# A log-sum-exp kernel on one core: a written order for the last six half-tiles, a bitwise check of the sums, and a store of its own for one column of results

## The chip, the cores and the metric

The kernel runs on one core of one Trainium2 chip. The metric is the device time of one execution in microseconds; three runs of the kernel before gave 322.96, 323.04 and 323.05. Engines are named as in the profile: PE is TensorE, DVE is VectorE, ACT is ScalarE, POOL is GpSimd, SP is SyncE, which here only issues DMAs. An engine works through its own instructions in order and waits on semaphores for the others.

## The reference

`x` has 8 x 2048 x 2048 float32, `bias` 8 x 256. Each row of 2048 is 8 heads of 256. For every row and head, the log of the sum of exponentials of `x + bias` over the 256 elements is wanted, and each result stands twice in the output of 8 x 8 x 4096 float32.

```python
x_heads = x.reshape(B, S, H, Dh).transpose(0, 2, 1, 3)
x_heads = x_heads + bias[None, :, None, :]
x_tiled = np.repeat(x_heads, 2, axis=2)
mx = x_tiled.max(axis=-1, keepdims=True)
lse = mx.squeeze(-1) + np.log(np.exp(x_tiled - mx).sum(axis=-1))
```

## The kernel before

**The work.** The 16384 rows of `x` are taken in 64 tiles of 128 partitions x 2 rows x 2048 (a row of a tile is 128 x 2048 float32, 1 MB, and one head of it 128 x 256, 128 KB). "Row 62.1" is row 1 of tile 62. A batch has eight tiles, the last batch is tiles 56 to 63. The kernel sums exponentials without subtracting a maximum, and checks at the end whether the sums stayed in a safe range; if not, `all_again` (from L674) computes everything once more in the safe way. With this input it doesn't run.

**Four ways to do a head.** The bias can be added before the exponential, by TensorE: a matmul puts the bias into a PSUM bank, a second one with the identity adds `x` ("add", L831), and ScalarE takes the exponential out of PSUM, either with the sum in the same instruction ("sum", `sum_biased`, L480) or without ("copy", L842). Or the exponential is taken first, in place ("exp", `exp_inplace`, L505), and multiplied by the exponential of the bias afterwards: VectorE multiplies and sums in one instruction per head ("weigh", L540), or GpSimd multiplies (step 0, L557) and folds the head in halves down to 32 elements (steps 1 to 3, L563) and VectorE sums the rest ("folded", L570). A head that was copied out of PSUM is folded from step 1 on, without the multiplication.

**Stages.** Tiles 0 to 53 share the heads out in one way, 54 to 56 in another, 57 and up row by row (`PROMPT_F1`: two heads by TensorE, five weighed, one folded). From `T_TAIL` (62 before) on, the order is written out by hand: `TAIL_LOADS` lists the loads as (tile, row, first head, last head + 1), and `TAIL` the operations in the order in which they are issued. A word such as `weigh a:3` is head 3 of row a, and `fold a:01.1` step 1 for heads 0 and 1; a to d are the rows of `ROWS`. Since every engine is in order, this list sets the order on each engine; between engines semaphores do. `sums`, `rest`, `bits`, `limit` and `warm` stand for work left over from tile 61, for parts of the check, and for a matmul without a use of its own.

**PSUM.** Two pairs of banks (`pairs`) serve the adds in turn. `next_bias` (L800) puts the bias of the next "add" of the list into the next bank as soon as the add before it is issued. TensorE waits there until ScalarE has read what was in the bank.

**Queues.** All loads and the stores of the results of batches 0 to 6 (`store`, L601) are issued by SyncE, in order, on one queue (q1 in the profile); at most eight transfers are outstanding, since each new one waits for the one eight before it. The bias, its three bf16 parts (L316) and the last store (L750) are issued by ScalarE on another queue (q10).

**The end.** The sums of the last batch stand in `R_last`, 128 partitions x 128 columns (head, tile of the batch, row). `finish_last` (L740) transposes them on TensorE, takes the logarithm (L749) into `res_last`, and stores 128 rows of 256 float32 from ScalarE (L750). `judge` (L657) subtracts the bits of 1.0 from the bits of the last sums (L627), takes the largest absolute value with that of the earlier ones (L645), adds it up over the partitions with a matmul (L665), and changes the type (L666); every engine loads the verdict (L667) and branches (L956). The earlier sums were treated by `off_seen` on GpSimd and `limit_seen` on VectorE. Then each engine waits at the end of the program, SyncE for all outstanding transfers too (L983).

Of the kernel before, what the change touches and what calls it, by code (L numbers as in the profile page):

```python
# [40 lines left out]
ONE_BITS = 127 << 23  # L41
SPAN_BITS = 60 << 23
# [8 lines left out]
T_TAIL = 62  # L51
# [15 lines left out]

ROWS = {"a": (62, 0), "b": (62, 1), "c": (63, 0), "d": (63, 1)}


TAIL = """
add a:01  sums  add a:2  warm
exp a:3-7
rest  bits
weigh a:3  weigh a:4  weigh a:5  weigh a:6  weigh a:7
exp d:4-7
copy a:01
sum a:2
fold a:01.1  fold a:01.2  fold a:01.3
add b:2  # L80
exp b:3-7
weigh d:4  weigh d:5  weigh d:6  weigh d:7
sum b:2
add c:1
exp c:2-4
fold b:67.0  fold b:67.1  fold b:67.2  fold b:67.3
weigh b:3  weigh b:4  weigh b:5
add b:0
exp b:1
sum c:1  # L90
exp c:5-7
weigh c:2  weigh c:3  weigh c:4  weigh b:1
add c:0
sum b:0
exp d:3
folded a:01  limit
weigh c:5  weigh c:6  weigh c:7
sum c:0
exp d:1
add d:0  add d:2  # L100
weigh d:3  weigh d:1
sum d:0
sum d:2
folded b:67
# [4 lines left out]
def kernel(  # L109
# [44 lines left out]
    off = sb.tile([P, 1 + 2 + NR + H * SEEN], F32, name="off")  # L154
    off_last = sb.tile([P, H * LATE + 1], F32, name="off_last")
    far = sb.tile([P, 1], BF16, name="far")
    scale_bf = sb.tile([P, 1], BF16, name="scale_bf")
    verdict = sb.tile([1, 1], I32, name="verdict")
# [26 lines left out]
    sb.tile([P, 24], F32, name="gap")  # L185
# [19 lines left out]
    def rows_of(t, n=1):  # L205


        b, at = divmod(t, NBLK)
        if b < B - 2:
            blk, i = divmod(at, TB)  # L210
            v = x[b, blk * P * KB : (blk + 1) * P * KB, :]
            return v.rearrange("(p k) d -> p k d", k=KB)[:, i * K : (i + n) * K]
        v = x[b, at * P * K : (at + 1) * P * K, :]
# [119 lines left out]
    nc.vector.memset(Rx[0][:, 0:1], 1.0)  # L333
    nc.vector.memset(Rx[0][:, 1 + widths[0] :], 1.0)
    nc.vector.memset(off[:, 0:1], float(SPAN_BITS))
    nc.vector.memset(scale_bf, 2.0**-8)
# [32 lines left out]
    def on_bank(i, ins, banks=1):  # L369
        here = range(i, i + banks)  # L370
        for at, u in bank_users[i // 2]:
            if not set(at) & set(here) and u.ins.engine != ins.ins.engine:
                tc.declare_no_dep(ins.ins, u.ins, reason="another bank")
        bank_users[i // 2].append((here, ins))
        return ins
# [176 lines left out]
    def fold_step(t, k, h0, h1, step, after):  # L552


        v = xts[t % NBUF][:, k, h0 * Dh : h1 * Dh]
        if step == 0:
            done = nc.gpsimd.tensor_tensor(  # L557
                out=v, in0=v, in1=w_sb[:, h0 * Dh - W1 : h1 * Dh - W1], op=ALU.mult
            )
            return on_x(t, done, [after])  # L560
# [5 lines left out]
        return on_x(t, done, [after])  # L566

    def add_folded(t, k, h0, h1, sums, done):
        v = xts[t % NBUF][:, k, h0 * Dh : h1 * Dh]
        red = nc.vector.tensor_reduce(  # L570
            out=sums[:, k, h0:h1],
            in_=v.rearrange("p (h j) -> p h j", j=Dh)[:, :, 0:FOLD],
            op=ALU.add,
            axis=mybir.AxisListType.X,
        )
        on_x(t, red, [done])

    def fold(t, k, h0, h1, sums, after):
        step = 0
        while Dh >> step >= FOLD:  # L580
            after = fold_step(t, k, h0, h1, step, after)
            step += 1
        return lambda: add_folded(t, k, h0, h1, sums, after)
# [42 lines left out]
    def off_one(engine, to, bits):  # L626
        engine.tensor_scalar(  # L627
            out=to,
            in0=bits,
            scalar1=-1.0 * ONE_BITS,  # L630
            scalar2=None,
            op0=ALU.add,
        )
# [4 lines left out]
    def off_seen():  # L638
        n = 1 + 2 + NR
        off_one(nc.gpsimd, off[:, 1:n], Rx[len(groups)].bitcast(I32))  # L640
        to = off[:, n:].rearrange("p (h c) -> p h c", h=H)
        off_one(nc.gpsimd, to, last_bits(0, SEEN))

    def farthest(to, of):
        nc.vector.tensor_reduce(  # L645
            out=to,
            in_=of,
            op=ALU.max,
            axis=mybir.AxisListType.X,
            apply_absolute_value=True,  # L650
        )

    def limit_seen():
        n = H * LATE
        farthest(off_last[:, n : n + 1], off)

    def judge():  # L657


        n = H * LATE  # L660
        to = off_last[:, 0:n].rearrange("p (h c) -> p h c", h=H)
        off_one(nc.vector, to, last_bits(SEEN, NBLK * K))
        farthest(far, off_last)
        total = tp[0:1, 0, 0:1]
        nc.tensor.matmul(total, lhsT=far, rhs=scale_bf, start=True, stop=True)  # L665
        nc.vector.tensor_copy(verdict, total)  # L666
        return nc.values_load(  # L667
            verdict,
            min_val=0,
            max_val=(1 << 31) - 1,  # L670
            skip_runtime_bounds_check_because="it is only compared, and addresses nothing",
        )
# [67 lines left out]
    def finish_last():  # L740
        bank = n_ps[0] % len(ps)
        last = ps[bank][:, 0:P]
        nc.tensor.transpose(
            out=last, in_=R_last.rearrange("p h n k -> p (h n k)"), identity=ident
        )
        tv = bass.AP(
            tensor=last.tensor, offset=last.offset, ap=[last.ap[0], [1, P], [0, 2]]
        )
        nc.scalar.activation(out=res_last, in_=tv, func=ACT.Ln)  # L749
        nc.scalar.dma_start(  # L750
            out=out[B - 1].rearrange("h (n r) -> (h n) r", r=2 * P),
            in_=res_last.rearrange("q p r -> q (p r)"),
        )


    def sums_of(t):

        b, blk = divmod(t, NBLK)
        if b < B - 2:
            return R[b][:, blk % TB * K :, :, blk // TB]  # L760
        if b == B - 2:
            return R[b][:, :, :, blk]
        return R_last[:, :, blk, :].rearrange("p h k -> p k h")
# [20 lines left out]
    for word in TAIL.replace("  ", "\n").split("\n"):  # L784
# [5 lines left out]
        if "-" in heads:  # L790
            heads = [h for h in range(int(heads[0]), int(heads[-1]) + 1)]
        else:
            heads = [int(h) for h in heads]
# [5 lines left out]

    def next_bias():  # L800
        if not to_bias:
            return
        row, heads = to_bias.pop(0)

        if len(heads) > 1:
            n_ps[0] += n_ps[0] % 2
        bank = n_ps[0] % len(ps)
        n_ps[0] += 1
        n = len(heads) * Dh
# [14 lines left out]
    def tail_step(what, t, k, heads, step):  # L824
# [4 lines left out]
        if what == "add":  # L829
            bank, c = biased[(t, k), heads[0]]  # L830
# [4 lines left out]
            next_bias()  # L835
        if what == "sum":
            (h,) = heads
            bank, c = biased[(t, k), h]
            sum_biased(t, k, h, bank, in_ps(bank, c, Dh), made["add", t, k, h], sums)
        if what == "copy":  # L840
            bank, c = biased[(t, k), heads[0]]
            act = nc.scalar.activation(out=v, in_=in_ps(bank, c, n), func=ACT.Exp)  # L842
            mms = [made["add", t, k, h] for h in heads]
            on_bank(bank, on_x(t, act, mms), banks=(c + n + MM - 1) // MM)
# [6 lines left out]
        if what == "weigh":  # L851
            (h,) = heads
            weigh(t, v, h, dst, made["exp", t, k, h])
        if what == "fold":
            after = made.get(("fold", t, k, heads[0])) or made["exp", t, k, heads[0]]
            done = fold_step(t, k, heads[0], heads[-1] + 1, step, after)
            made["fold", t, k, heads[0]] = done
        if what == "folded":
            add_folded(t, k, heads[0], heads[-1] + 1, sums, made["fold", t, k, heads[0]])

    for t in range(T_TAIL):
# [4 lines left out]
        for k0, k1, c0, c1 in pieces(t):  # L866
# [6 lines left out]
            else:  # L873
                heads = add_x(m, t, k0, c0, c1, bias_here)

                def pe_part(t=t, heads=heads, sums=sums):
                    for k, h, bank, p, mm in heads:
                        sum_biased(t, k, h, bank, p, mm, sums)

            if not m["late"]:  # L880
                if next_units:
                    bias_there = put_bias(*next_units.pop(0))
                else:
                    next_bias()
# [10 lines left out]
            if h0 < h1 and not m["late"]:  # L895
# [5 lines left out]
                if hf < h1:  # L901
                    for_pool.append(fold(t, k0, hf, h1, sums, done))
# [25 lines left out]
            else:  # L928
                for_pe.append(pe_part)
# [9 lines left out]
        if t == T - 3:  # L939
            store()  # L940
    for what, row, heads, step in tail:
        if row is None:
            {
                "sums": lambda: flush(for_pe),
                "rest": lambda: flush(for_pool),
                "bits": off_seen,
                "limit": limit_seen,
                "warm": keep_warm,
            }[what]()
            continue  # L950
        tail_step(what, *row, heads, step)
    finish_last()
    again = judge() > SPAN_BITS // 2

# [33 lines left out]
```

## Time and profile before

| what | us |
|---|---|
| median of three runs | 323.04 |
| the profiled execution | 322.96 |
| its span, first to last instruction | 321.2 |
| DVE / ACT / POOL / PE busy, of the span | 286.9 / 264.2 / 287.2 / 246.3 |
| last issue of a load (SP) | 309.3 |
| last sum on ACT / on DVE ends | 317.20 / 317.57 |
| verdict written (DVE L666) | 318.50 |

The span is the time from the first to the last instruction; 1.8 us of the execution lie around it. The profile is one execution; times within it are counted from the start of the span. In a timeline the columns are: start, duration, engine, line, operation, what it writes and reads, count, and in brackets how long the engine stood idle before and who released it. An instruction's duration reaches into the next one's where the engine overlaps them, so the cost of one in a row of them is the distance from start to start. In the DMA view of a stretch, a queue's line gives its packets, MB, and the time of its packets as a share of 16 engines over the stretch. "DMA to landing" is from the issue to the last semaphore increment.

### The profile page before, as it was taken

The numbers are of one execution on the slowest core, as the hardware profiler recorded it, in microseconds if no ns is written. First come the engines' busy times: TensorE is split into PE (matmuls) and PEld (weight loads), VectorE is DVE, ScalarE is ACT, GpSimd is POOL, SyncE is SP. The second block draws the span as 40 slices with busy tenths as digits, with TensorE's granted clock in tenths as the row PEclk, the third lists the DMA queues.
The fourth block names the chain that finished last, engine by engine and source line by source line (L and its number), as shares of the span: only waits on it lengthen the run. The fifth ranks groups of instructions, "written<-read, shape, count | busy, mean of one in ns | idle before, by whom it ended". The sixth has DMA issues, their size and how long they took to land.

```text
span 321.2 us, 2277 instructions
## 1 busy us (share of the span) xinstructions
PE 246.3 (77%) x611; PEld 99.2 (31%) x612; DVE 286.9 (89%) x308; ACT 264.2 (82%) x436; POOL 287.2 (89%) x118
## 2 busy tenths in 40 slices
PE   5998787867866979866697786677877688398873
PEld 2333332323322323322233332232333233143331
DVE  1339998799999699999979999999999999999986
ACT  1169868888888697988869998889888998999995
POOL 7939997999999999999999999999999999977773
PEclk9999977999997897999869999999999999979998
DMA  7999999999999999999999999999999999999994
GB/s 297 460 420 457 400 450 443 404 457 437 412 457 417 428 451 400 453 441 413 449 434 420 449 418 433 424 426 431 433 435 432 422 435 432 417 429 427 426 411 188
DMA packets 8806, 135.44 MB, mean 422 GB/s; under 512 B 980, under 2 KB 1495, under 8 KB 2519
## 3 DMA queue, kind: packets, MB, share of 16 engines
q1 hardware_dynamic: 8640, 135.14, 98.4%
q10 hardware_dynamic: 152, 0.14, 0.1%
q8 instruction: 5, 0.08, 0.1%
q14 instruction: 9, 0.07, 0.1%
HBM read 134.23 MB, written 1.05 MB: 421 GB/s over the span
## 4 chain that ended last, share of the span: by engine, by line
DMA 48%; POOL 15%; DVE 14%; ACT 10%; PE 10%; issue 0%; SPq 0%; DVEq 0%
DMA xb<-in_x_dram 48%; POOL xb L499 15%; DVE R L524 10%; ACT xb L505 6%; PE pair L449 4%; PE one_ps L449 2%; DVE xb L540 2%; ACT xb L467 2%; DVE xb L517 2%; PE pair L391 1%; PE pair L321 1%; ACT xb L460 1%; PE one_ps L391 1%; DMA brow<-in_bias_dram 1%; ACT xb L480 0%
## 5 line engine op out<-in xcount | busy, mean ns | idle before, releaser
L499 POOL TENSOR_TENSOR xb<-xb,b_rep 128x2048 f32<-128x2048 f32 x57 | 257.6, 4547 | 19.0 <-DMA xb<-in_x_dram 18.9
L524 DVE TENSOR_REDUCE R<-xb 128x14 f32<-128x3584 f32 (+1 forms) x57 | 216.8, 3803 | 2.5 <-ACT xb L505 0.6
L505 ACT ACTIVATE xb<-xb 128x2560 f32<-128x2560 f32 (+5 forms) x78 | 156.3, 2014 | 19.1 <-POOL xb L499 19.0
L449 PE MATMUL pair<-xb,ident 128*128 128x512 f32 x216 | 109.5, 632 | 0.0
L449 PE MATMUL one_ps<-xb,ident 128*128 128x512 f32 x108 | 62.4, 662 | 16.3 <-DMA xb<-in_x_dram 16.2
L467 ACT ACTIVATE xb<-pair 128x1024 f32<-128x1024 f32 x54 | 55.5, 1028 | 17.5 <-PE pair L449 17.5
L449 PEld LDWEIGHTS pair<-xb,ident 128*128 128x128 f32 x216 | 44.3, 205 | 57.9 <-issue 57.9
L517 DVE TENSOR_TENSOR xb<-xb,w_ps 128x512 f32<-128x512 f32 x54 | 36.7, 680 | 21.2 <-ACT xb L505 21.1
L391 PE MATMUL one_ps<-b,ones_bf 128*128 128x512 bf16 x52 | 20.1, 387 | 39.8 <-ACT xb L460 39.7
L460 ACT ACTIVATE xb<-one_ps 128x256 f32<-128x256 f32 x108 | 39.9, 378 | 7.1 <-PE one_ps L449 7.1
L391 PEld LDWEIGHTS <-ones_bf 128*128 128x128 bf16 (+1 forms) x174 | 17.6, 101 | 88.4 <-issue 81.8
L391 PE MATMUL pair<-b,ones_bf 128*128 128x512 bf16 x104 | 31.2, 381 | 0.0
L449 PEld LDWEIGHTS one_ps<-xb,ident 128*128 128x128 f32 x108 | 19.6, 199 | 31.4 <-DMA xb<-in_x_dram 25.2
L426 PE MATMUL pair<-xb,ident 128*128 128x512 f32 x32 | 18.5, 679 | 8.2 <-DMA xb<-in_x_dram 8.2
L540 DVE CUSTOM_DVE_ANT_0 xb<-xb,w_ps 128x256 f32<-128x256 f32 x61 | 22.5, 417 | 0.4 <-ACT xb L505 0.4
L460 ACT ACTIVATION_READ_ACCUMULATOR xb<-one_ps 128x1 f32 x108 | 22.0, 204 | 0.0
L563 POOL TENSOR_TENSOR xb<-xb 128x128 f32<-128x128 f32 (+3 forms) x36 | 13.5, 375 | 3.9 <-ACT xb L842 1.1
L480 ACT ACTIVATE xb<-pair 128x256 f32<-128x256 f32 x39 | 15.0, 407 | 0.0
L557 POOL TENSOR_TENSOR xb<-xb,w_sb 128x256 f32<-128x256 f32 (+1 forms) x11 | 8.5, 777 | 3.7 <-ACT xb L505 3.0
L426 PEld LDWEIGHTS pair<-xb,ident 128*128 128x128 f32 x32 | 5.7, 205 | 16.8 <-DMA xb<-in_x_dram 14.8
L480 ACT ACTIVATION_READ_ACCUMULATOR xb<-pair 128x1 f32 x39 | 9.1, 233 | 0.0
L440 PE MATMUL tp<-b_rep,ident 128*128 128x384 f32 x22 | 8.9, 486 | 0.0
(64 smaller groups left out, 82.0 us busy)
## 6 DMA issues: line engine op xcount, KB each, us to landing
xb<-in_x_dram SPq DMA_DIRECT2D x20, 4096.0 KB, 22.4
xb<-in_x_dram SPq DMA_DIRECT2D x17, 2048.0 KB, 21.9
xb<-in_x_dram SPq DMA_DIRECT2D x11, 1024.0 KB, 22.1
xb<-in_x_dram SPq DMA_DIRECT2D x2, 512.0 KB, 17.5
xb<-in_x_dram SPq DMA_DIRECT2D x1, 768.0 KB
xb<-in_x_dram SPq DMA_DIRECT2D x2, 256.0 KB, 10.5
out_dram<-res SPq DMA_DIRECT2D x1, 512.0 KB
xb<-in_x_dram SPq DMA_DIRECT2D x1, 384.0 KB, 13.2
```

The lines of the kernel that those rows point to most:

```text
L391: nc.tensor.matmul(p, lhsT=lhsT, rhs=each_row(b, h * Dh, Dh, K), start=i == 0, stop=False,)
L426: mm = nc.tensor.matmul(p, lhsT=ident, rhs=xts[t % NBUF][:, ka:kb, c : c + w], start=False, stop=True,)
L449: mm = nc.tensor.matmul(p, lhsT=ident, rhs=xts[t % NBUF][:, :, h * Dh : (h + 1) * Dh], start=False, stop=True,)
L460: act = nc.scalar.activation(out=xts[t % NBUF][:, k, 0:Dh], in_=got[0][:, k * Dh : (k + 1) * Dh], func=ACT.Exp, accum_out=sums[:, k, 0:1],)
L467: act = nc.scalar.activation(out=xts[t % NBUF][:, :, Dh : m["pe"] * Dh].rearrange("p k (h j) -> p h k j", j=Dh), in_=got[-1].rearrange("p ...
L480: act = nc.scalar.activation(out=xts[t % NBUF][:, k, h * Dh : (h + 1) * Dh], in_=p, func=ACT.Exp, accum_out=sums[:, k, h : h + 1],)
L499: add = nc.gpsimd.tensor_tensor(out=v, in0=v, in1=each_row(b_rep, c - G0, D - c, k1 - k0), op=ALU.add)
L505: return on_x(t, nc.scalar.activation(out=v, in_=v, func=ACT.Exp), [after])
L517: mul = nc.vector.tensor_tensor(out=f, in0=f, in1=each_row(w_ps, m["pe"] * Dh - W0, n, k1 - k0), op=ALU.mult,)
L524: red = nc.vector.tensor_reduce(out=sums[:, k0:k1, h0:H], in_=v.rearrange("p k (h j) -> p k h j", j=Dh), op=ALU.add, axis=mybir.AxisListTy ...
L540: ttr = nc.vector.tensor_tensor_reduce(out=v, in0=v, in1=w, scale=1.0, scalar=0.0, op0=ALU.mult, op1=ALU.add, accum_out=dst,)
L563: done = nc.gpsimd.tensor_tensor(out=v[:, :, 0:n], in0=v[:, :, 0:n], in1=v[:, :, n : 2 * n], op=ALU.add)
```

## The change

- `T_TAIL` is 61 instead of 62: the written order now covers rows 61.0 to 63.1, six rows named e, f, a, b, c, d, with 14 loads where tile 61 had two and the list ten. Row c is now 63.1 and row d 63.0; the last head to arrive is head 0 of row d. Sums, copies, folds and products are shared out anew among the engines. A new word `whole` is a plain reduction on VectorE of a head that was copied out of PSUM.
- `next_bias` looks whether the bank that is next has been read by all that the list lets read it (`to_read`), and otherwise waits for a later word of the list; it is tried after every word.
- The blocks of the last batch are read in reverse order (`rows_of`, `sums_of`), so that row d's head 0 is column 0 of the sums.
- The check: a bitwise AND and a bitwise XOR in one VectorE instruction per group of sums (`odd_bits`) leave zero where a sum's top bits are the usual ones. `gather` adds the results, read as bf16, over the partitions with matmuls of at most 128 columns into one PSUM row: the earlier sums at `seen`, the last in `judge`. One reduction with absolute values gives the verdict, which is read as an integer. GpSimd's part, `limit_seen` and the change of type are gone.
- The end: `finish_last` is gone. `finish_one` takes the logarithm of column 0 as it stands, 128 partitions x 1, and stores it from ScalarE, two floats per partition. `finish_rest` transposes the other 127 columns, takes their logarithm, and stores 127 rows of 256 float32 from SyncE. In the list `final` (the first) stands ahead of `main` (the second), and both ahead of `judge`.
- `store` is called after the loop; on SyncE's queue it stands behind all loads, as before. Two memsets of the start go, two have another value; tile sizes and the unused tile `gap` change.

```diff
-T_TAIL = 62
+T_TAIL = 61
...
 TAIL_LOADS = [
-    (62, 0, 0, 8),
-    (63, 1, 4, 8),
-    (62, 1, 2, 8),
-    (63, 0, 1, 5),
-    (62, 1, 0, 2),
-    (63, 0, 5, 8),
+    (61, 0, 0, 8),
+    (61, 1, 0, 5),
+    (63, 1, 0, 8),
+    (61, 1, 5, 8),
+    (62, 0, 0, 6),
+    (62, 1, 5, 8),
+    (63, 0, 2, 7),
+    (62, 1, 0, 1),
+    (62, 0, 6, 8),
+    (62, 1, 1, 3),
+    (62, 1, 3, 5),
+    (63, 0, 1, 2),
+    (63, 0, 7, 8),
     (63, 0, 0, 1),
-    (63, 1, 0, 1),
-    (63, 1, 3, 4),
-    (63, 1, 1, 3),
 ]
...
+ROWS = {"e": (61, 0), "f": (61, 1), "a": (62, 0), "b": (62, 1), "c": (63, 1), "d": (63, 0)}
...
+add e:01  exp e:34567
+add e:2  copy e:01  weigh e:3  exp f:234  add f:01  warm
+fold e:01.1  weigh e:4  weigh e:5  copy e:2
+weigh e:6  fold e:01.2  sums  weigh e:7  copy f:01  fold e:01.3  weigh f:2
+sums  weigh f:3  fold f:01.1  exp c:34567  weigh f:4
+add c:12  whole e:2  fold f:01.2  folded e:01  rest  seen6
+fold f:01.3  exp f:567  seen7  weigh c:3  fold c:67.0  add c:0  weigh c:4
+sum c:1  weigh c:5  seen  sum c:2  weigh f:5
+copy c:0  weigh f:6  add a:12  exp a:345  fold c:67.1  weigh f:7
+whole c:0  exp b:567  folded f:01  fold c:67.2  weigh a:3  add a:0
+weigh a:4  fold c:67.3  copy a:12  weigh a:5  weigh b:5  sum a:0
+fold a:12.1  weigh b:6  add d:2  exp d:3456  weigh b:7
+fold a:12.2  add b:0  folded c:67  exp a:67  weigh d:3  fold d:6.0
+weigh d:4  sum d:2  add b:12  weigh d:5  sum b:0  fold a:12.3  weigh a:6
+exp b:34  fold d:6.1  weigh a:7  sum b:1  add d:1  folded a:12  fold d:6.2
+weigh b:3  exp d:7  weigh b:4  fold d:6.3  add d:0  sum b:2  weigh d:7
+sum d:1  folded d:6  sum d:0
+final  main
...
-    nc.vector.memset(off[:, 0:1], float(SPAN_BITS))
-    nc.vector.memset(scale_bf, 2.0**-8)
...
+    def odd_bits(to, bits):
+        nc.vector.tensor_scalar(
             out=to,
             in0=bits,
+            scalar1=TOP_BITS,
+            scalar2=USUAL_BITS,
+            op0=ALU.bitwise_and,
+            op1=ALU.bitwise_xor,
         )
...
+    odd_ps = tp[0:1, KB - 1]
+
+    def gather(bits, start, stop):
+        v = bits.bitcast(BF16)
+        n = v.shape[1]
+        for c in range(0, n, P):
+            w = min(P, n - c)
+            nc.tensor.matmul(
+                odd_ps[:, 0:w],
+                lhsT=ones_bf[:, 0:1],
+                rhs=v[:, c : c + w],
+                start=start and c == 0,
+                stop=stop,
+            )
+
+    def see_before():
+        odd_bits(odd[:, 0 : 2 + NR], Rx[len(groups)].bitcast(I32))
+
+    def see_early():
+        to = odd[:, 2 + NR :].rearrange("p (h c) -> p h c", h=H)
+        odd_bits(to, last_bits(LATE, NBLK * K))
+
+    def judge():
+        to = odd_last.rearrange("p (h c) -> p h c", h=H)
+        odd_bits(to, last_bits(0, LATE))
+        gather(odd_last, False, True)
         nc.vector.tensor_reduce(
+            out=verdict,
+            in_=odd_ps,
             op=ALU.max,
             axis=mybir.AxisListType.X,
             apply_absolute_value=True,
         )
...
-    def finish_last():
+    def finish_rest():
         bank = n_ps[0] % len(ps)
...
+        n = P - 1
+        rest = ps[bank][0:n, 0:P]
+        nc.tensor.transpose(out=rest, in_=sums_in[-1][:, 1:], identity=ident)
         tv = bass.AP(
...
+        nc.scalar.activation(out=res_last[0:n], in_=tv, func=ACT.Ln)
+        nc.sync.dma_start(
+            out=out[B - 1].rearrange("h (n r) -> (h n) r", r=2 * P)[1:],
+            in_=res_last[0:n].rearrange("q p r -> q (p r)"),
+        )
+
+    def finish_one():
+        one = sums_in[-1][:, 0:1]
+        tv = bass.AP(tensor=one.tensor, offset=one.offset, ap=[one.ap[0], [0, 2]])
+        nc.scalar.activation(out=res_one, in_=tv, func=ACT.Ln)
         nc.scalar.dma_start(
+            out=out[B - 1, 0, 0 : 2 * P].rearrange("(p r) -> p r", r=2), in_=res_one
         )
...
     def next_bias():
-        if not to_bias:
+        bank = n_ps[0] % len(ps)
+        if not to_bias or ahead or to_read[bank]:
             return
         row, heads = to_bias.pop(0)
...
+        if what == "whole":
+            red = nc.vector.tensor_reduce(
+                out=dst, in_=v, op=ALU.add, axis=mybir.AxisListType.X
+            )
+            on_x(t, red, [made["exp", t, k, heads[0]]])
...
-    finish_last()
-    again = judge() > SPAN_BITS // 2
+    again = judge() > 0
```

More of the change, by code (lines that the diff above doesn't have):

```diff
@@ L40 @@
 BIAS_MAX = 20.0
[L41 to L42 removed]
+TOP_BITS = -(1 << 28)
+USUAL_BITS = 1 << 30
 TOO_FAR = 3.0e38
@@ L153 @@
     LATE = NBLK * K - SEEN
[L154 to L158, printed above, removed]
+    odd = sb.tile([P, 2 + NR + H * SEEN], I32, name="odd")
+    odd_last = sb.tile([P, H * LATE], I32, name="odd_last")
+    verdict = sb.tile([1, 1], F32, name="verdict")
     starts = [0]
@@ L367, with on_bank @@
     bank_users = [[], []]
[L369 to L372, printed above, removed]
+    def on_bank(i, ins):
+        for j, u in bank_users[i // 2]:
+            if j != i and u.ins.engine != ins.ins.engine:
                 tc.declare_no_dep(ins.ins, u.ins, reason="another bank")
-        bank_users[i // 2].append((here, ins))
+        bank_users[i // 2].append((i, ins))
         return ins
@@ L559, in fold_step @@
             )
-            return on_x(t, done, [after])
+            return on_x(t, done, after)
         v = v.rearrange("p (h j) -> p h j", j=Dh)
@@ L565, in fold_step @@
         )
-        return on_x(t, done, [after])
+        return on_x(t, done, after)
     def add_folded(t, k, h0, h1, sums, done):
@@ L575, in add_folded @@
         )
-        on_x(t, red, [done])
+        on_x(t, red, done)
     def fold(t, k, h0, h1, sums, after):
@@ L651, in farthest @@
         )
[L653 to L666, printed above, removed]
         return nc.values_load(
-            verdict,
+            verdict.bitcast(I32),
             min_val=0,
@@ L789 @@
         heads, _, step = heads.partition(".")
[L790 to L793, printed above, removed]
+        heads = [int(h) for h in heads]
         tail.append((what, ROWS.get(row), heads, int(step or 0)))
@@ L829, in tail_step @@
         if what == "add":
+            next_bias()
+            assert ahead.pop() == ((t, k), heads)
             bank, c = biased[(t, k), heads[0]]
@@ L842, in tail_step @@
             act = nc.scalar.activation(out=v, in_=in_ps(bank, c, n), func=ACT.Exp)
-            mms = [made["add", t, k, h] for h in heads]
-            on_bank(bank, on_x(t, act, mms), banks=(c + n + MM - 1) // MM)
+            on_bank(bank, on_x(t, act, [made["add", t, k, heads[0]]]))
+            to_read[bank] -= len(heads)
             for h in heads:
@@ L853, in tail_step @@
             weigh(t, v, h, dst, made["exp", t, k, h])
+        if what == "whole":
[3 more added lines that the diff above has]
+            on_x(t, red, [made["exp", t, k, heads[0]]])
         if what == "fold":
-            after = made.get(("fold", t, k, heads[0])) or made["exp", t, k, heads[0]]
+            after = [made["exp", t, k, h] for h in heads]
+            if ("fold", t, k, heads[0]) in made:
+                after = [made["fold", t, k, heads[0]]]
             done = fold_step(t, k, heads[0], heads[-1] + 1, step, after)
@@ L858, in tail_step @@
         if what == "folded":
-            add_folded(t, k, heads[0], heads[-1] + 1, sums, made["fold", t, k, heads[0]])
+            done = made["fold", t, k, heads[0]]
+            add_folded(t, k, heads[0], heads[-1] + 1, sums, [done])
     for t in range(T_TAIL):
@@ L874, with pe_part @@
                 heads = add_x(m, t, k0, c0, c1, bias_here)
-                def pe_part(t=t, heads=heads, sums=sums):
-                    for k, h, bank, p, mm in heads:
-                        sum_biased(t, k, h, bank, p, mm, sums)
+                pe_parts = [
+                    lambda t=t, one=one, sums=sums: sum_biased(t, *one, sums)
+                    for one in heads
+                ]
+                def pe_part(pe_parts=pe_parts):
+                    flush(pe_parts)
             if not m["late"]:
@@ L901 @@
                 if hf < h1:
-                    for_pool.append(fold(t, k0, hf, h1, sums, done))
+                    for_pool.append(fold(t, k0, hf, h1, sums, [done]))
             flush(for_pe)
@@ L938, with sum_before @@
             finish_two()
-        if t == T - 3:
-            store()
+    store()
+    last_bank = heads[0][2]
+    to_read[last_bank] = len(for_pe)
+    def sum_before():
+        for_pe.pop(0)()
+        to_read[last_bank] -= 1
+    next_bias()
     for what, row, heads, step in tail:
@@ L943 @@
             {
-                "sums": lambda: flush(for_pe),
+                "sums": sum_before,
                 "rest": lambda: flush(for_pool),
-                "bits": off_seen,
-                "limit": limit_seen,
+                "seen6": see_before,
+                "seen7": see_early,
+                "seen": lambda: gather(odd, True, False),
                 "warm": keep_warm,
+                "main": finish_rest,
+                "final": finish_one,
             }[what]()
-            continue
-        tail_step(what, *row, heads, step)
-    finish_last()
-    again = judge() > SPAN_BITS // 2
+        else:
+            tail_step(what, *row, heads, step)
+        next_bias()
+    assert not for_pe and not for_pool and not to_bias
+    again = judge() > 0
     order.__exit__(None, None, None)
```

83 lines of the change are left out of this document (16 added, 67 removed).

## The prediction

> **What bounds the kernel now.** I read the page's table of DMA first, then the chain that ended last, then the timeline of ScalarE and TensorE over the last ten microseconds, then the waits of SyncE and the DMA view of the first 20 and last 5 us. The page:
>
> ```profile
> DMA  7999999999999999999999999999999999999994
> ...
> DMA packets 8806, 135.44 MB, mean 422 GB/s; under 512 B 980, under 2 KB 1495, under 8 KB 2519
> ...
> q10 hardware_dynamic: 152, 0.14, 0.1%
> ```
>
> The 16 DMA engines are full until the last slice, so the body runs at the rate of the loads, and the change touches neither their bytes nor the work up to tile 60. What it can move lies behind about 303 us. The end, from the timelines of ScalarE and TensorE:
>
> ```profile
> 316.31 0.44 ACT L480 ACTIVATE xb<-pair 128x256 f32<-128x256 f32 x1
> 316.57 0.26 ACT L480 ACTIVATION_READ_ACCUMULATOR xb<-pair 128x1 f32 x1
> 316.67 0.45 ACT L480 ACTIVATE xb<-pair 128x256 f32<-128x256 f32 x1
> 316.93 0.27 ACT L480 ACTIVATION_READ_ACCUMULATOR xb<-pair 128x1 f32 x1
> 318.06 0.38 ACT L749 ACTIVATE res_last<-pair 128x256 f32<-128x256 f32 x1 [0.85 <-PE pair L743]
> 318.47 0.39 ACTq L750 DMA_DIRECT2D out_dram<-res_last  x1
> ...
> 315.60 0.70 PE L831 MATMUL pair<-xb,ident 128*128 128x256 f32 x2
> 317.72 0.30 PE L743 MATMUL pair<-ident,R 128*128 128x128 f32 x1 [1.43 <-DVE R L570]
> ```
>
> The last load is in at 315.6 (the matmul at 315.60 starts on it). ScalarE is done at 317.20, VectorE's last sum at 317.58; transpose, logarithm and the store's issue at 318.47 follow. The store lands 1.8 us after its issue, and 0.9 us of barrier follow: 318.47 + 1.8 + 0.9 = 321.2, the span. That the store and not the verdict ends the run is in SyncE's waits, where the verdict's path (read at 318.5) is through before it:
>
> ```profile
> SPq L667 <- DVE verdict L666: 5.0, 1, 5.0
> SPq L983 <- PEq L983: 0.6, 2, 0.5
> SPq L983 <- DMA out_dram<-res_last: 0.3, 1, 0.3
> ```
>
> So whatever delays the landing of the last store delays the end one for one, and there is nothing behind which it can hide.
>
> **The new stores: how many engines they use.** The old last store has 128 rows of 1 KB. The new one leaves out row 0 (head 0 of tile 63, row half 0): 127 rows of 1 KB, on SyncE's queue. The DMA view of the last 5 us and of the first 20 us, ScalarE's queue q10 alone:
>
> ```profile
> q10 hardware_dynamic: 144, 0.13, 7.7%
> ...
> q10 hardware_dynamic: 8, 0.01, 0.3%
> ```
>
> The first is the 128-row store: 128 packets of data and 16 small ones, one for each engine that took part. The second is two transfers of one row (the bias) and three rows (its bf16 parts): 4 packets of data and 4 small ones, that is 1 and 3 engines. The page fits: SyncE issues 60 transfers of 64 or 128 rows (20+17+11+2+1+2+1+3 loads, 3 stores), 60 x 16 + 16 + 1 + 3 = 980, exactly the packets under 512 B. Every transfer whose rows I can count shares them evenly: 128 as 16 x 8, 64 as 16 x 4, 3 as 3 x 1, 1 as 1 x 1. 127 is prime: the only even share on at most 16 engines is all 127 rows on one. No row of the trace has a row count that 16 doesn't divide and that is above 16, so this cost has two ends: shared nearly as 128 rows (8 on the busiest engine), no added cost; or 127 on one. I take one engine, because even shares are the one pattern that all 63 transfers keep, and the three-row store, which left 13 engines idle rather than cut a row, is the nearest odd count.
>
> [...]
>
> Price of a 1 KB packet: 7.7% of 16 engines over 5 us is 6.16 us for 128 packets and 16 small ones, about 47 ns each. On one engine the store has 127 - 8 = 119 more of them in a line: 119 x 47 ns = 5.6 us. Bounds: at the rate of the large loads (135.14 MB in 98.4% of 16 x 321.2 us, 38 ns per KB) 4.5 us; at the rate of the small transfers at the start (0.3% of 16 x 20 us = 0.96 us for 12.5 KB, 77 ns per KB) 9.2 us.
>
> The other new store (128 rows of 8 bytes, ScalarE's queue) has 16 engines and is issued earlier; its packets are shorter than 1 KB, so I give it at most the 1.8 us of the old one. It is covered by the store that follows.
>
> **When the 127-row store is issued.** ScalarE does the exponentials of the tail without a break in both lists, so I compare lists from 303.30 on (both start with an exp of row 61.0). Start to start in the timeline, a sum costs 0.36 us, a copy of 512 columns 0.48 (310.50 to 310.98), an exp 0.10 + 0.215 per head (0.31 for one, 1.16 for five). Before: 13 sums, one copy of 512, 10 exps with 35 heads. After: 11 sums, three copies of 512, two of 256 (0.28 each, my estimate between the 0.26 that the sum's ACTIVATE takes and 0.31), 10 exps with 31 heads. Difference: -2 x 0.36 + 2 x 0.48 + 2 x 0.28 - 4 x 0.215 = -0.06 us. So ScalarE's last sum, now head 0 of the last row, is done at 317.15. Its data are in time: the list has 14 loads for 12, four of one head for three, and a 1 KB packet costs 47 ns where 1 KB of a large one costs 38, 8 per engine, so some 0.15 us later than 315.60; with the matmul's 0.70 that is 316.45, and ScalarE reaches this sum at 316.6.
>
> Then on ScalarE, one behind another: the logarithm of one column (0.25, from the 0.38 of 256 columns less most of its length), the issue of the small store (0.39, as L750), the logarithm of the 127 rows (0.38): 317.15 + 0.04 + 0.25 + 0.39 + 0.38 + 0.03 = 318.25, where SyncE issues. The transpose that the second one needs waits for the other 127 sums. VectorE ends these earlier: 28 products for 31 (0.343 each, -1.0), two reductions of one head (0.3 each), three more small folded sums (0.13), two bit operations of 130 and 80 elements (between 0.18, the old 32-wide one, and 0.55, GpSimd's 130-wide one, so 0.4 to 1.0 for both), without the reduction to a limit (0.30): about even in work, but not waiting for the final sum, it ends near 316.9. TensorE gets the added matmuls of the check: 4 of at most 128 columns, between 0.1 and 0.38 each (the 512-column bf16 row): at the upper end row 62.0's add is late by up to 1 us, which ScalarE could feel as 0.4 us; I take 0 and keep 0.4 for the range. GpSimd's folds (five chains) leave idle time.
>
> The check: one reduction and one small type change less, verdict about 0.5 us sooner. The read of the verdict was covered by the store already (the 0.3 us above), so it is worth nothing. SyncE now issues the store before it reads the verdict, 0.4 to 0.5 us later; with the store on one engine that too is covered, otherwise both ways end together. The output stores behind the loads and the two memsets less at the start cost nothing: the queue has drained by 317.8 (old landings 5 us after 311.1 to 313.0), and VectorE's first work waits for data. The rows of the last batch are read in reverse order, the same bytes.
>
> **Sum.** Issue -0.2 us (318.47 to 318.25), landing +5.6: +5.4 us. The profiled execution took 322.96 us (span 321.2 and 1.8 around it), the median is 323.04, within 0.1. 322.96 + 5.4 = **328.4 us**, span 326.6.
>
> **Rivals.**
> 1. *127 rows spread over all engines, seven or eight each.* For it: nothing in the trace forbids an uneven share. Against: none is seen. Then the landing is 1.8 us after 318.25, and the time is 322.96 - 0.2 = 322.8: not slower. What decides is one count, the small packets of that store, 16 or 1. Chance 0.10, of which 0.02 for a list that gains more than 0.65 us.
> 2. *The list itself runs dry.* ScalarE waits where a load or an add is late (six adds of the tail wait for loads in the profile before, 4.6 us in all), with the store spread. It has to lose 0.85 us to end over 0.65 slower: 323.8. Chance 0.03.
> 3. *The store isn't one transfer of 127 rows*, but cut in two (64 and 63 rows, say; 63 shares as 9 x 7). It would land under half a microsecond later than the old one: 323.3. Chance 0.02.
> 4. *One engine* (my forecast): chance 0.85.
>
> **How the numbers follow.** A difference under 0.2% (0.65 us) is about what a measurement of this kernel can't tell from no change. Slower: 0.85 + 0.03 = 0.88; within: 0.08 of rival 1 and rival 3, 0.10; faster: 0.02. The range is that of the one-engine case: the packet's bounds give 322.96 - 0.2 + 4.5 = 327.3 and 322.96 - 0.2 + 9.2 = 332.0; ScalarE's list may add 0.4 or take 0.3. 327.0 to 332.0 holds nearly all of 0.85, so about 8 in 10.
>
> **What would show it.** The DMA view of the last microseconds: SyncE's queue with 127 packets of 1 KB and one small one behind them, a share of about one sixteenth (0.06) for some 6 us, and "DMA to landing" of the new store near 7.4 us where the old had 1.8. SyncE's (or another queue's) last long wait is for res_last, 5 us or more, and all engines are idle behind 318.7. ScalarE's last sum ends within 0.4 us of 317.15, the store is issued within 0.5 of 318.25, the verdict is there before 318.2. I am wrong if that store lands within 2.5 us of its issue; then the time is near 322.8. I am wrong on the list if ScalarE shows idle gaps that sum to over 0.5 us between 303 and 317.

## The result, and the profile after

The changed kernel takes 328.82 us (median of 6 runs, 328.44 to 329.76) against 323.05 (322.93 to 323.33): a ratio of 1.0182, interval 1.0171 to 1.0193. It is 5.8 us slower; forecast was 328.4. The profiled execution is the longest of the six, 329.76 us with a span of 328.0, so its profile shows 6.8 us more than the one before, a microsecond more than the medians do.

The page after, the table of DMA and the packet counts:

```profile
DMA  7999999999999999999999999999999999999970
...
DMA packets 9222, 135.44 MB, mean 413 GB/s; under 512 B 1141, under 2 KB 1783, under 8 KB 3063
...
q10 hardware_dynamic: 152, 0.01, 0.0%
```

The loads fill the engines as before; the last slice, of 8.2 us, is nearly empty now, where before it stood at 4 tenths. The small packets can be counted again: SyncE issues 59 loads and 3 stores of results with 16 small packets each (992), ScalarE's three transfers have 16 + 1 + 3 = 20, the new store of one column brings 128 pieces of 8 bytes, and 992 + 20 + 128 = 1140. One is left for the store of 127 rows: it ran on one engine. SyncE's queue alone, from 318.5 to 327 us, says the same, 127 packets of data and one small one:

```profile
q1 hardware_dynamic: 128, 0.13, 5.1%
```

The DMA view from 318 us to the end (40 slices of a quarter of a microsecond, then packets, MB, share of 16 engines):

```profile
GB/s 25 8 0 0 4 0 0 12 8 57 20 37 12 12 25 25 25 4 0 25 25 20 25 25 25 25 25 25 25 25 25 20 25 12 0 0 0 0 0 0
...
q10 hardware_dynamic: 144, 0.00, 0.8%
...
out_dram<-res_last SPq DMA_DIRECT2D x1, 127.0 KB
out_dram<-res_one ACTq DMA_DIRECT2D x1, 1.0 KB, 4.2
```

From 319.8 to 326.4 us the core moves some 20 GB/s on average and 25 in most slices, with one engine at work on the store; the old store ran at 262 to 360 from 319.4 to 319.75. The last column is the time from issue to landing: the 8-byte store took 4.2 us, though it is 1 KB in all. The view gives none for the 127-row store, since it works from 16 increments of a transfer's semaphore and this one has fewer. The trace keeps their times, though: the 128-row store of before had 16 increments, from 320.04 to 320.23, and this one has two, one at 319.46, ahead of its first packet, and one at 326.71. SyncE's waits say the same:

```profile
SPq L1009 <- DMA out_dram<-res_last: 6.1, 1, 6.1
SPq L743 <- ACT res_last L742: 3.5, 1, 3.5
```

SyncE reached the barrier's waits at 320.5 and stood 6.1 us for the store, where the old one cost it 0.3. The store was issued at 319.02 and landed at 326.71: 7.7 us, where it was 1.8. ScalarE's end shows when it could be issued (L465 is the sum, L753 the logarithm of the column, L742 that of the 127 rows):

```profile
317.43 0.39 ACT L465 ACTIVATE xb<-pair 128x256 f32<-128x256 f32 x1
317.69 0.22 ACT L465 ACTIVATION_READ_ACCUMULATOR xb<-pair 128x1 f32 x1
317.94 0.20 ACT L753 ACTIVATE res_one<-R 128x2 f32<-128x2 f32 x1
318.17 0.39 ACTq L754 DMA_DIRECT2D out_dram<-res_one  x1
318.61 0.38 ACT L742 ACTIVATE res_last<-pair 127x256 f32<-127x256 f32 x1 [0.47 <-PE tp L633]
...
317.96 0.38 PE L738 MATMUL pair<-ident,R 128*127 128x128 f32 x1 [0.70 <-ACT xb L465]
```

The 6.8 us of the two profiles, then: the last store is issued at 319.0 instead of 318.47 (0.55), takes 7.7 us instead of 1.8 (5.9), and the end follows 1.25 us behind its landing instead of 0.95 (0.3). The waits named on the last two lines mislead a little. The second logarithm is put down to a matmul of the check, but ScalarE was issuing the small store until 318.56. The transpose does wait for ScalarE, and for the last head's sum, which it doesn't read.

### The profile page after: what moved, and what is told of

It reads as the page before. It is cut to its first block, busy times and chain, and to the rows that moved or that the text cites. A ratio compares the mean times of both kernels' runs of the same rounds, so it can differ in the third digit from the quotient of the medians.

```text
span 328.0 us, 2286 instructions
## 1 busy us (share of the span) xinstructions
PE 248.3 (76%) x618; PEld 100.1 (31%) x618; DVE 287.4 (88%) x303; ACT 264.7 (81%) x437; POOL 287.6 (88%) x118
## 4 chain that ended last, share of the span: by engine, by line
DMA 57%; POOL 22%; ACT 7%; DVE 6%; PE 3%; SPq 1%; issue 0%; ACTq 0%
DMA xb<-in_x_dram 57%; POOL xb L484 22%; ACT xb L490 5%; DVE R L509 5%; PE pair L434 2%; PE one_ps L434 1%; DVE xb L502 1%; ACT xb L465 1%; ACT xb L452 1%; SPq L234 0%; ACT xb L445 0%; DVE R L604 0%; PE one_ps L309 0%; SPq L249 0%; ACT xb L847 0%
## 5 line engine op out<-in xcount | busy, mean ns | idle before, releaser
L490 ACT ACTIVATE xb<-xb 128x2560 f32<-128x2560 f32 (+6 forms) x78 | 155.3, 2000 | 18.9 <-POOL xb L484 18.3
L548 POOL TENSOR_TENSOR xb<-xb 128x128 f32<-128x128 f32 (+3 forms) x39 | 15.5, 400 | 4.8 <-ACT xb L847 2.0
L465 ACT ACTIVATE xb<-pair 128x256 f32<-128x256 f32 x37 | 14.0, 397 | 0.0
L836 PE MATMUL pair<-xb,ident 128*128 128x256 f32 (+1 forms) x24 | 9.5, 490 | 2.3 <-DMA xb<-in_x_dram 2.3
L542 POOL TENSOR_TENSOR xb<-xb,w_sb 128x256 f32<-128x256 f32 (+1 forms) x10 | 7.8, 784 | 3.0 <-ACT xb L490 2.5
L465 ACT ACTIVATION_READ_ACCUMULATOR xb<-pair 128x1 f32 x37 | 8.3, 224 | 0.0
```

The source lines that it names most:

```text
L465: act = nc.scalar.activation(out=xts[t % NBUF][:, k, h * Dh : (h + 1) * Dh], in_=p, func=ACT.Exp, accum_out=sums[:, k, h : h + 1],)
L490: return on_x(t, nc.scalar.activation(out=v, in_=v, func=ACT.Exp), [after])
L548: done = nc.gpsimd.tensor_tensor(out=v[:, :, 0:n], in0=v[:, :, 0:n], in1=v[:, :, n : 2 * n], op=ALU.add)
```

## The experiments

The kernel before was run beside each (322.98 to 323.02 us in these sets). Ratios are to it; the two kernels with one run have none. Where a landing is given "by the increments", it is the time of the last increment in the trace.

**The 127 rows cut in two.** The changed kernel with

```diff
-            out=out[B - 1].rearrange("h (n r) -> (h n) r", r=2 * P)[1:],
-            in_=res_last[0:n].rearrange("q p r -> q (p r)"),
+        rows = out[B - 1].rearrange("h (n r) -> (h n) r", r=2 * P)[1:]
+        for q0, q1 in ((0, 112), (112, 127)):
+            nc.sync.dma_start(
+                out=rows[q0:q1],
+                in_=res_last[q0:q1].rearrange("q p r -> q (p r)"),
```

> The changed kernel, its 127-row store cut into 112 and 15 rows, two transfers on SyncE's queue. Theory (rows are shared out evenly, the engines taken are a divisor of the row count): 16 and 15 engines, the second store lands within 2.5 us of its issue, where the 127 rows took 7.7; the time falls by about 5 us to 322.8 if the 8-byte store (4.2 us from issue to landing in the changed kernel) was only held up by the 127-row one, and to 324.2 if its 4.2 us are its own, since it is then the last to land. Rival (the list, the check or the two stores as such cost the time): within 1 us of 328.8.

Measured: 325.46 us, ratio 1.0074 (1.0061 to 1.0088). 3.4 us of the 5.8 are gone, which the rival excludes; but it stops short of both values of the theory. The DMA view from 317.2 to 323 us (slices of 0.145 us; q14 fetches instructions):

```profile
GB/s 71 14 0 0 0 0 2 6 0 0 0 0 92 240 275 149 177 14 56 0 0 0 0 0 0 0 0 0 0 0 7 0 0 0 0 0 0 0 0 0
...
q14 instruction: 2, 0.02, 4.3%
...
out_dram<-res_last SPq DMA_DIRECT2D x1, 112.0 KB
out_dram<-res_one ACTq DMA_DIRECT2D x1, 1.0 KB, 4.1
out_dram<-res_last SPq DMA_DIRECT2D x1, 15.0 KB, 3.9
```

The 8-byte store's 4.1 us don't come from the 127-row store, then. And the two others, issued 0.8 and 1.3 us behind it, took 4.2 (by the increments) and 3.9 us for 7 and 1 packets on an engine, which was not expected. Nearly all their packets had started by 319.8, as the first row shows; what is late is the landing, from 321.6 to 322.5, behind the last of the 8-byte store's at 321.4.

**125 and 2 rows.** The same with the cut at 125.

```diff
-        for q0, q1 in ((0, 112), (112, 127)):
+        for q0, q1 in ((0, 125), (125, 127)):
```

> The changed kernel, its 127-row store cut into 125 and 2 rows. Theory of divisors: 125 = 5 x 25, five engines, so 25 packets of about 50 ns in a line instead of 7 in the cut at 112: the store lands about 0.9 us later than there, near 3 us after its issue, and the time is 0 to 0.9 us above that kernel's. Rival (any row count above 16 that 16 doesn't divide goes on one engine): within 0.5 us of the changed kernel, 328.8. Rival (shared unevenly over all engines): as the cut at 112.

Measured: 325.61 us, ratio 1.0079 (1.0064 to 1.0094), 0.15 above the cut at 112. SyncE's queue in the DMA view from 318 to 325.5 us, of this kernel and then of the cut at 112:

```profile
q1 hardware_dynamic: 134, 0.13, 5.8%
```

```profile
q1 hardware_dynamic: 158, 0.13, 6.0%
```

Both have 127 packets of data. The small ones left are 7 here and 31 there: 5 + 2 engines for 125 and 2 rows, 16 + 15 for 112 and 15. So the number of engines is a divisor of the rows, and not "16 or one". The 0.9 us expected for 25 packets in a line did not show at the end: the last packet started at 320.46, where with the cut at 112 all but one had started by 319.75, but the store landed 4.1 us after its issue, nearly as the 112 rows did, hidden in the same delay behind the 8-byte store.

**The old end on the new list.** The written list, the bitwise check and all else of the changed kernel, with `finish_last` of before:

```diff
-final  main
+last
...
-                "main": finish_rest,
-                "final": finish_one,
+                "last": finish_last,
```

> The changed kernel with the end of before: all 128 columns are transposed, logged and stored in one store of 128 rows from ScalarE; the written list and the bitwise check stay. Theory: no store on one engine is left, so the time is 322.3 to 323.0, and what it differs by from before (323.05) is the list and the check alone. Rival (the list costs the time): near 328.

Measured: 322.95 us, ratio 0.9999 (0.9990 to 1.0008): the two stores are the whole loss, and list and check together are worth nothing that shows. Yet in its profile, of an execution of 322.75 us, the last store was issued at 317.81, 0.66 us earlier than before. SyncE's waits at its end:

```profile
SPq L661 <- DVE verdict L654: 3.2, 1, 3.2
SPq L1023 <- DMA out_dram<-res_last: 0.9, 1, 0.9
```

The landing is at 319.56, the end at 320.88: 1.32 us behind it, where before it was 0.96. So 0.36 of the 0.66 us went behind the landing.

**The 127-row store alone, in the kernel before.**

```diff
-        nc.scalar.dma_start(
-            out=out[B - 1].rearrange("h (n r) -> (h n) r", r=2 * P),
-            in_=res_last.rearrange("q p r -> q (p r)"),
-        )
+        rows = out[B - 1].rearrange("h (n r) -> (h n) r", r=2 * P)
+        for q0, q1 in ((1, P), (0, 1)):
+            nc.scalar.dma_start(
+                out=rows[q0:q1],
+                in_=res_last[q0:q1].rearrange("q p r -> q (p r)"),
+            )
```

> The kernel before with one edit: its last store of 128 rows is cut into rows 1 to 127 and row 0, both from ScalarE. Theory: the 127 rows go on one engine, 119 packets of 52 ns more in a line, 6.2 us: 329.2, and the store lands 7.5 to 8 us after its issue where it took 1.8. Rival (the store alone is harmless, the list costs the time): 323.1 to 323.5.

Measured: 328.54 us, ratio 1.0167 (1.0153 to 1.0181). One row taken out of a store of 128, and stored by itself behind it, costs 5.5 us in a kernel that is otherwise the old one. The DMA view from 318.4 to 327 us, and SyncE's wait:

```profile
q10 hardware_dynamic: 130, 0.13, 4.7%
```

```profile
SPq L985 <- DMA out_dram<-res_last: 5.0, 1, 5.0
```

130 packets are 127 + 1 of data and two small ones: one engine each. By the increments the 127 rows landed 7.1 us after their issue and the one row 0.2 us behind them. 7.14 is 5.4 more than the 1.76 of before, at 119 packets more 45 ns each, a little under the 52 that I expected from the changed kernel.

**The column as one row.** The cut at 112, and head 0's column transposed first and stored as one row of 1 KB:

```diff
-        one = sums_in[-1][:, 0:1]
...
+        nc.tensor.transpose(out=one, in_=sums_in[-1][:, 0:1], identity=ident)
...
-            out=out[B - 1, 0, 0 : 2 * P].rearrange("(p r) -> p r", r=2), in_=res_one
+            out=out[B - 1, 0:1, 0 : 2 * P], in_=line
```

> The kernel with the store cut at 112, and the column of its own transposed first, so that it is stored as one row of 1 KB instead of 128 pieces of 8 bytes; all else as there. Theory (the 8-byte pieces are slow to land and hold up what the same engines write behind them, 2.5 us of 325.46 against 322.95 with the old end): the 112-row store lands about 2 us after its issue instead of 4.2, the one-row store within 2.5; the transpose and the longer logarithm cost up to 0.6: 323.2 to 324.0. Rival (a second small store on another queue costs it, whatever its form): 325 to 326.

Measured: 324.59 us, ratio 1.0053 (1.0037 to 1.0068). By the increments the row landed 1.1 us after its issue and the 112 rows 1.9 after theirs, where with the 8-byte pieces it was 4.1 and 4.2. So the form of the small store is what held the others up. The instruction fetches show it too: two of 8 KB took 4.0 us together with the 8-byte store (4.3% of 16 engines over 5.8 us, above) and 0.8 here (5.5 us):

```profile
q14 instruction: 2, 0.02, 0.9%
```

The time is 0.6 above the range expected: the column's logarithm now waits for a transpose and the big store is issued at 318.65 in this profile, and of the two transfers the 15-row one is the last, issued 0.4 us later still and 2.4 us on its way:

```profile
out_dram<-res_last SPq DMA_DIRECT2D x1, 15.0 KB, 2.4
```

**The big store ahead of the small one.** The cut at 112, with `main  final` for `final  main` in the list; one run.

> The kernel with the store cut at 112, and the store of the 127 columns issued ahead of the 8-byte store instead of behind it. Theory (the 8-byte writes hold up those behind them on the same engines): the 112-row store lands about 2 us after its issue instead of 4.2, the 8-byte store still some 4 us after its own, the time stays at 325.0 to 326.0. Rival (SyncE's queue is slow here by itself): 4 us for the 112 rows in either order.

Measured: 327.21 us, above the 325.0 to 326.0 expected. In this execution the transpose waited for VectorE until 318.27, and both queues issued at nearly the same time, 319.06 and 319.16, so the order asked for was hardly there. By the increments, 11 of the 112-row store's 16 came within 1.7 us, the other five after 2.3 to 4.8:

```profile
out_dram<-res_one ACTq DMA_DIRECT2D x1, 1.0 KB, 4.9
out_dram<-res_last SPq DMA_DIRECT2D x1, 15.0 KB, 4.5
```

That most of one store came early and the rest late speaks against a queue that is slow by itself. That the 8-byte writes delay what the same engines write is the author's estimate; the views don't tell the engines apart. The question of the order stays open.

**The transpose into another pair of banks.** The changed kernel; one run:

```diff
     def finish_rest():
-        bank = n_ps[0] % len(ps)
+        bank = (n_ps[0] + 1) % len(ps)
```

> The changed kernel, one edit: the transpose of the 127 columns goes to a bank of the other pair than the last head's add. Theory (in the changed kernel the transpose waited for the last head's sum, 0.70 us, although it doesn't read it, because its bank lies in the pair that this sum reads): it now starts when head 1's sum is written, about 0.35 us ahead of the end of the last head's sum, and the time stays within 0.6 us of 328.8, since ScalarE takes the small logarithm and the small store first. Rival (the sums' tile is tracked as a whole): the transpose still starts after the last head's sum.

Measured: 328.35 us, span 326.6. TensorE and ScalarE at its end:

```profile
316.75 0.35 PE L738 MATMUL pair<-ident,R 128*127 128x128 f32 x1 [0.41 <-ACT xb L465]
...
316.78 0.21 ACT L465 ACTIVATION_READ_ACCUMULATOR xb<-pair 128x1 f32 x1
```

The transpose now starts 0.24 us ahead of the end of the last sum (316.99), where it started behind it. The wait came from the shared pair. It brings nothing, since ScalarE's two earlier steps stand in front of the logarithm anyway. This execution, which doesn't have the profiled one's late loads, also shows the plain sizes: issue at 318.10, 7.2 us to the landing.

**Where the 0.66 us of the list went.** SyncE waits for the eight transfer semaphores at the end in a fixed order, 0.06 us from one to the next where all have come. Transfers take them in turn, so how many come before decides which one the last store gets: in the kernel before the seventh of the order, in the changed kernel the second, with the new list and the old end the first. Two kernels move it to the last place by leaving out one transfer; both have the new list, the new check and the old end. In the first, heads 0 and 1 to 2 of row 62.1 come in one load behind 62.0's last:

```diff
-    (62, 1, 0, 1),
     (62, 0, 6, 8),
-    (62, 1, 1, 3),
+    (62, 1, 0, 3),
```

> The list and the check of the changed kernel with the end of before, and one load less (62.1 heads 0 and 1 to 2 in one transfer behind 62.0 heads 6 to 7). Theory: that kernel's last store was issued 0.66 us earlier than before's (317.81 against 318.47) and the time stayed the same, since SyncE, which waits for the eight transfer semaphores in a fixed order of some 0.06 us each, had seven waits still to do behind the store's where before had one; one transfer less moves the store to the last semaphore of that order: 0.4 us less, 322.5. Rival (the list's own end sets the time, or the later head 0 delays it): 322.9 to 323.3.

Measured: 323.06 us, ratio 1.0012 (0.9996 to 1.0028): no gain (one of the eleven runs took 325.92, the others 322.89 to 323.37). In its profile the end does follow the landing after 0.87 us instead of 1.32, but the store is issued only at 318.73. The tail (row 61.0's first exp on ScalarE) began 0.34 us later there than with the list's own loads (303.55 against 303.21), and ScalarE waited 0.35 for an add on the later load:

```profile
314.95 0.38 ACT L464 ACTIVATE xb<-pair 128x256 f32<-128x256 f32 x1 [0.35 <-PE pair L850]
```

In the second the list's loads stay, and tiles 42 and 43 come in one load in the middle of the kernel:

```diff
-BLOCKS = 42
+BLOCKS = 44
```

> The list and the check of the changed kernel with the end of before, all 14 loads of the list as they were, and one transfer less in the middle of the kernel: tiles 42 and 43 come in one load of 4 MB instead of two of 2 MB. Theory (SyncE's fixed order of waits): the last store moves from the first semaphore of that order to the last, so the barrier's end follows the landing after 0.9 us instead of 1.3, and the time falls by 0.4 us, to 322.5. Rival (the order of waits is nothing, or the bigger load delays the loads behind it): 322.9 or more.

Measured: 322.86 us, ratio 0.9993 (0.9984 to 1.0002). The store landed at 319.72 and the span ended at 320.59, 0.87 us behind, and SyncE's wait is down from 0.9 to 0.3:

```profile
SPq L1023 <- DMA out_dram<-res_last: 0.3, 1, 0.3
```

The mechanism is there in the profile, 0.45 us of it (0.87 instead of 1.32); in the medians it is 0.1, less than the runs of this kernel differ among themselves (322.33 to 323.26). Whether this version beats the kernel before is not settled. No version tried is clearly faster than it.

## Why the prediction was right, point by point

- *127 rows go on one engine.* Right, and shown twice: one small packet for that store, and 5.5 us in the old kernel from its last store alone. The pattern of even shares from rows of 1, 3, 64 and 128 held for 127, 125, 112, 15 and 2, with 1 small packet for 127 rows, 7 for 125 and 2, and 31 for 112 and 15.
- *5.6 us for 119 packets of 47 ns.* Right: 5.4 in the old kernel, 5.5 with the other pair of banks, 5.9 in the profiled execution (each landing less 1.76).
- *Issued at 318.25, 0.2 us earlier.* Right in size where the loads came as expected: 318.14 with the cut at 112 and 318.10 with the other pair. In the profiled execution it was 319.0. Its tail began 0.25 us late, and the loads behind came later still: the last one landed at 316.51, where it was 315.56 before and I had 0.15 more. ScalarE stood idle for 0.3 us in all. This is where the profile is longer than the medians; why the loads were late there, the trace doesn't settle. With the other pair of banks and with the old end the last of the same 14 loads landed at 315.59 and 315.57, so the smaller loads cost nothing there.
- *The signs.* The 7.4 us to the landing, SyncE's long wait and the packets of its queue came as said. In the profiled execution three others did not: the last sum ended at 317.91 (within 0.4 of 317.15 was said), the store was issued 0.77 us past 318.25 (0.5 was said), the verdict was written at 318.79 (318.2 was said). With the other pair of banks all three hold: 316.99, 318.10, 317.79.
- *ScalarE's lists cost the same.* Right: from 303.2 to the last sum at 317.0 in the kernel with the old end, 13.8 us without an idle gap, where the sum over the rows gave 13.85. VectorE's last sum there ended at 316.6, where I had 316.9.
- *The 8-byte store lands within 1.8 us.* Wrong: 4.2. "Its packets are shorter than 1 KB" was no bound, since no row of the trace had a store of such pieces. It was covered, as I had it, by the 127-row store. With the cut at 112 that cover is gone, and the new end costs 2.5 us (325.46 against 322.95 with the old end); stored as one row, with a transpose more, it costs 1.6 (324.59). How much of the rest is the cut and how much the second store, no run separates.
- *The transpose waits for the other 127 sums only.* Wrong: it waited for the last head's as well, through its pair of banks. It cost nothing, as ScalarE was busy.
- *0.9 us behind the landing.* It was 1.25, off by 0.35: the order of SyncE's waits, and 0.96 was the value before.
- *The check's shorter way is worth nothing.* Right: SyncE stood 6.1 us for the store behind the verdict.
- *The rivals.* An uneven share over all engines is excluded by the one small packet. The list that runs dry happened in part in the profiled execution, where the store was issued 0.55 us later than before, and doesn't set the result. A cut store was priced at 323.3. The rows are shared as was said, but the time was 325.46, since the 8-byte store held up the landing, and 324.59 with one row in its place.

In the execution with the other pair of banks the sum comes out at the forecast's span, 326.6, with three small errors in it: the issue 0.15 us earlier, 0.2 less on the way (7.2 where 1.8 + 5.6 was forecast), 0.35 more behind the landing. That these cancel is luck, and it is one run; the median of the changed kernel is 0.4 us above the forecast.

## What to carry to other kernels

Count the rows of a store before taking one away: 128 rows on sixteen engines and 127 on one differ by 119 packets in a line, 5.4 to 5.9 us here, and at the end of a kernel nothing covers it. A result that is ready early was not worth a store of its own here (324.59 us with it as one row, 322.95 without it), in pieces of 8 bytes least of all (325.46). Work that is saved ahead of the last store is worth only what the barrier behind it passes on; in the profile with the old end 0.36 of 0.66 us went into its fixed order of waits. When one cost covers another (here the one-engine store the 8-byte one), removing the first shows the second, so price both before promising the sum.

## What the runs showed of the hardware that was not expected

A store of 128 pieces of 8 bytes (1 KB in all) took 4.2 us to land in the changed kernel, 4.1 and 4.0 with the cuts at 112 and 125 rows and 4.9 with the order turned, against 1.76 for 128 KB in pieces of 1 KB in the kernel before. Its pieces don't start late: with the cut at 112 all 128 started between 318.18 and 318.37, and the 16 increments came one after another from 318.68 to 321.38. Stores of 112 and 125 rows issued 0.8 us behind it took 4.2 and 4.1 us, and 1.9 (112 rows) when the small store was one row. Fetches of 8 KB of instructions that started while it was landing took 1.5 to 2.3 us each (2.28 and 2.29 in the changed kernel), and 0.3 to 0.5 in the kernels without it (0.46 and 0.49 in the one before). With the cut at 112 it was the landing of the 112-row store that was late, not its packets: 30 of the 31 small packets of SyncE's queue had started by 319.8, and the store's increments came between 321.59 and 322.31, all behind those of the 8-byte pieces. The slow fetches are no increments, so the delay is not in the increments alone. Why the pieces are slow to land, and how they hold up the others, no run here shows.
